# Adding transfers issued by GpSimd make the low halves of plainly split weights, in place of subtractions on VectorE

## The chip, the cores and the metric

The kernel runs on one core of one Trainium2 chip. The metric is device microseconds (us) of one execution. The kernel before took 1804.53, 1805.53 and 1805.5 us in three runs, median 1805.5 us.

## What is computed

Two transformer blocks, one after the other, on 512 positions of width 1024, all in float32 (the reference in JAX, cut):

```python
# first block
u = rms_norm(h, attn_pre_norm[i])
c_q, c_kv, k_rope, m_q, m_k, m_v, m_o, m_i, m_f = split_cols(u @ w_in[i], IN_SIZES)
...
mix = jnp.concatenate([mla_out, mlstm_out], axis=-1) @ w_out[i]
h = h + rms_norm(mix, attn_post_norm[i])
f = rms_norm(h, ffn_pre_norm[i])
f = (jax.nn.silu(f @ w_gate[i]) * (f @ w_up[i])) @ w_down[i]
h = h + rms_norm(f, ffn_post_norm[i])
h = h + jax.nn.sigmoid(h @ w_ple_gate[i]) * (p[i] @ w_ple_proj[i])
# second block, on 16 meta positions and these 512
for i in range(2):
    h = _rmsnorm(hres, norm_g[i, 0])
    m = _diff_attention(...) if i == 0 else _short_conv(...)
    hres = hres + _rmsnorm(m, norm_g[i, 1])
    h = _rmsnorm(hres, norm_g[i, 2])
    a = jax.nn.relu(h @ w_up[i])
    hres = hres + _rmsnorm((a * a) @ w_down[i], norm_g[i, 3])
```

## The kernel before, in words

**Split products.** TensorE multiplies in a reduced format (F32R). So that the product is good to float32, each weight and each activation is kept as two F32R halves, high and low (`x = hi + lo`), and `mm3` (lines 344, 345 and 346) issues three matmuls per tile: weight high by activation high, weight high by activation low, weight low by activation high. Line 346 alone reads a weight's low half.

**The weights.** They lie in HBM as float32, in pieces of [128, 1024] (768 wide for the last down projection of the first block). `loader` brings them in the order of use: each half of a piece, 128x512 or 256 KB, goes by one DMA that SP issues (`dma`, line 325) into one of six `raw` buffers. `converter` follows in the same order: ACT copies `raw` into the weight's high half, in F32R (`copy`, line 289), and a small stream of its own, `convert_lo`, makes the low half as `raw - hi` (`lo`, which calls `tt`, line 303; the planner gives it to VectorE, DVE, or to GpSimd, POOL). Then `convert_lo` gives the `raw` buffer back, and after both halves the weight counts as made. A made weight lies in one of five buffers `whl` or, while their pool is open, one of four buffers `whx`. PE frees it with its last matmul on it (`drop`). Some weights of the three FFNs are not split in this plain way but as "pair" or "part" pieces (`convert_pair`, `part`), which make their low halves in their own code.

**The stages.** `s.phase` is 0 in the first block up to its mixer's output, 1 from `block1_rest` on (output projection, SwiGLU FFN), and 2 from the gate `ple` on (per-layer gate, differential attention, squared-ReLU FFN, short convolution, squared-ReLU FFN).

**The order of the work.** All of it is planned in Python before anything is emitted. Every piece of work is a generator that yields requests for an engine with a cost in us, or for a key or a buffer; `Sched.step` takes the request that can start first (then by priority), and the instruction is emitted there. So each engine has one fixed order, and in it an instruction waits for its semaphores, and what stands behind it on that engine waits too. `s.port` is the planner's lock between POOL and those DVE operations that read two operands from SBUF.

In `ple` (the gate at the end of the first block) ACT computes a sigmoid from each gate projection `t`; DVE multiplies it with the projection `u` and frees `u` for PE. In `converter` the copies stand where the planner put them among the other work of ACT: squares for the norms (`sqt`), activations' high halves (`a`), moves from PSUM (`y`).

```python
    def convert_lo(s, name, lo, raw, hi, left, x):
        yield from s.lo(lo, raw, hi)
        s.put("raw")
        left[0] -= 1
        if not left[0] and ("w", name) not in s.keys:
            s.set(("w", name))
```

Of the kernel before, what the change touches and what calls it, by code (L numbers as in the profile page):

```python
# [10 lines left out]
F32 = mybir.dt.float32  # L11
# [3 lines left out]
ALU = mybir.AluOpType  # L15
# [69 lines left out]
class Sched:  # L85
# [84 lines left out]
    def start(s, st):  # L170
        r = st.req
        if r[0] == "vg":
            d, p = max(st.at("dve"), s.free["dve"]), max(st.at("pool"), s.free["pool"], s.port)
            if r[3]:
                d = max(d, s.port)
            return (p, "pool", r[2]) if p + r[2] <= d + r[1] + 0.2 else (d, "dve", r[1])
        cost = r[1] * (1.07 if r[0] == "pe" else 1.0)
        if r[0] == "act" and len(r) > 2 and r[2] in s.TABLES and r[2] not in s.SERVES[s.table]:
            cost += 1.28
        a = max(st.at(r[0]), s.free[r[0]])  # L180
        if r[0] == "pool" or r[0] == "dve" and r[-1] is True:
            a = max(a, s.port)
        return a, r[0], cost

    def step(s):
        best = None
        for st in s.ready:
            a, eng, cost = s.start(st)
            late = 0.5 if eng == "act" and cost > 1.28 and s.table else 0.0
            k = (a + late, st.prio() if callable(st.prio) else st.prio, st.t, st.seq)  # L190
            if best is None or k < best[0]:
                best = k, st, a, eng, cost
        if best is None:
            return False
        _, st, a, eng, cost = best
        s.ready.remove(st)
        s.now = a
        s.free[eng] = a + cost
        if (eng == "pool" or eng == "dve" and st.req[-1] is True):
            s.port = a + cost  # L200
        st.t = st.end = a + cost + LAT
        st.last = eng
        value = eng
        if eng == "act" and len(st.req) > 2 and st.req[2] in s.TABLES and st.req[2] not in s.SERVES[s.table]:
            s.table = s.TABLES[st.req[2]]
            value = "load"
        s.advance(st, value)
        return True
# [39 lines left out]
class Kern(Sched):  # L248
# [93 lines left out]
    def mm3(s, ps, wh, wl, xh, xl, start, stop, **k):  # L342
        mm = s.nc.tensor.matmul
        mm(ps, wh, xh, start=start, stop=False, **k)  # L344
        mm(ps, wh, xl, start=False, stop=False, **k)  # L345
        mm(ps, wl, xh, start=False, stop=stop, **k)  # L346
# [16 lines left out]
    def mm(s, ps, l, r, start=True, stop=True, passes=1):  # L363
        yield "pe", passes * size(ps) / 2400
        s.nc.tensor.matmul(ps, l, r, start=start, stop=stop)  # L365
# [84 lines left out]
    def converter(s):  # L450
        for i, (name, src, n) in enumerate(s.wq):
            if name[0][0] == "da":
                yield "key", "x_closed"
            if name[0][1:] == ("up", 0, 0) and not name[1]:
                s.reserve()
            more = i + 1 < len(s.wq) and s.wq[i + 1][0][0][1] in ("pair", "part")
            if name[0][1] == "pair":
                if name[1]:
                    yield from s.convert_pair(name[0], more)
                continue  # L460
            if name[0][1] == "part":
                yield "key", ("raw", name, 0)
                yield from s.part(name, s.raw.pop((name, 0)), True, more)
                continue
            yield "key", ("raw", name, 0)
            w, kind = yield from s.w_room()
            s.w[name] = (w, kind)
            s.wn += 1
            left = [len(range(0, n, 512))]
            for x in range(left[0]):  # L470
                m = min(512, n - 512 * x)
                yield "key", ("raw", name, x)
                raw = s.raw.pop((name, x))[:, :m]
                hi, lo = (w[:, j, 512 * x:512 * x + m] for j in range(2))
                yield from s.copy(hi, raw)
                low = s.convert_lo(name, lo, raw, hi, left, x)
                if i:
                    s.spawn(low)
                else:
                    yield from low  # L480
                    s.set(("w+", name) if x else ("w", name))

    def convert_lo(s, name, lo, raw, hi, left, x):
        yield from s.lo(lo, raw, hi)
        s.put("raw")
        left[0] -= 1
        if not left[0] and ("w", name) not in s.keys:
            s.set(("w", name))
# [1891 lines left out]
```

## Time and profile before

| | before |
|---|---|
| median of three runs | 1805.5 us (1804.53 to 1805.53) |
| profiled execution: its own time | 1807.18 us |
| profiled execution: span of the trace | 1805.4 us |
| PE (matmul) busy | 1780.7 us, 99% |
| DVE busy | 1358.4 us, 75% |
| ACT busy | 1008.2 us, 56% |
| POOL busy | 169.8 us, 9% |
| transfers issued by SP | 169.73 MB, 29.4% of the 16 DMA engines' span |

The profile was taken from one execution; all stretches below are of that one. PE is TensorE's matmul pipe, DVE VectorE, ACT ScalarE, POOL GpSimd, SP the engine that issues the DMAs before. A row of the timeline gives the start in us from the start of the span, the length in us, engine, line, operation, the program's names (buffer numbers left out), the shape and how many instructions of a kind in a row; what stands in brackets is the idle time just before and what ended it.

### The profile page before, as it was taken

The numbers are of one execution on the slowest core, as the hardware profiler recorded it, in microseconds if no ns is written. First come the engines' busy times: TensorE is split into PE (matmuls) and PEld (weight loads), VectorE is DVE, ScalarE is ACT, GpSimd is POOL, SyncE is SP. The second block draws the span as 40 slices with busy tenths as digits, with TensorE's granted clock in tenths as the row PEclk, the third lists the DMA queues.
The fourth block names the chain that finished last, engine by engine and source line by source line (L and its number), as shares of the span: only waits on it lengthen the run. The fifth ranks groups of instructions, "written<-read, shape, count | busy, mean of one in ns | idle before, by whom it ended". The sixth has DMA issues, their size and how long they took to land.

```text
span 1805.4 us, 33466 instructions
## 1 busy us (share of the span) xinstructions
PE 1780.7 (99%) x12610; PEld 1658.2 (92%) x12610; DVE 1358.4 (75%) x3066; ACT 1008.2 (56%) x2280; POOL 169.8 (9%) x193
## 2 busy tenths in 40 slices
PE   9999999999999999999999999999999999999997
PEld 7888898999999989999999999999999988889997
DVE  7878579788887858887596777787855378777784
ACT  8767666544445546776675444455522467444452
POOL 2021001000010102111000000001000000111100
PEclk9999999999999999999999999999999999999999
DMA  5324411333325321111222333332422032333331
GB/s 193 96 83 135 148 59 67 116 100 106 106 91 161 106 62 60 60 60 61 68 76 90 98 101 106 99 122 81 146 93 91 23 100 77 101 112 98 105 106 47
DMA packets 96219, 171.87 MB, mean 95 GB/s; under 512 B 12000, under 2 KB 15760, under 8 KB 96056
## 3 DMA queue, kind: packets, MB, share of 16 engines
q1 hardware_dynamic: 96056, 169.73, 29.4%
q8 instruction: 99, 1.62, 0.4%
q14 instruction: 64, 0.52, 0.1%
HBM read 165.92 MB, written 2.13 MB: 93 GB/s over the span
## 4 chain that ended last, share of the span: by engine, by line
PE 92%; DVE 5%; ACT 1%; DMA 1%; issue 1%; SPq 0%; DVEq 0%; ACTq 0%
PE u L344 17%; PE u L345 17%; PE u L346 17%; PE t L345 12%; PE t L346 12%; PE t L344 12%; PE t L2012 1%; DVE whl L303 1%; DVE ssum L303 1%; PE t L765 1%; DVE a L316 1%; DVE y L316 1%; DVE h L303 0%; PE t L365 0%; ACT y L289 0%
## 5 line engine op out<-in xcount | busy, mean ns | idle before, releaser
L344 PE MATMUL u<-a,whl 128*128 128x256 f32 (+3 forms) x1860 | 594.0, 319 | 1.8 <-ACT a L289 0.9
L346 PE MATMUL u<-a,whl 128*128 128x256 f32 (+3 forms) x1860 | 588.0, 316 | 0.0
L345 PE MATMUL u<-a,whl 128*128 128x256 f32 (+3 forms) x1860 | 587.4, 316 | 0.3 <-DVE a L316 0.3
L289 ACT ACTIVATE whl<-raw 128x512 fp32r<-128x512 f32 (+1 forms) x658 | 387.6, 622 | 323.0 <-PE u L346 133.3
L303 DVE TENSOR_TENSOR whl<-raw,whl 128x512 fp32r<-128x512 f32 x625 | 430.1, 708 | 129.6 <-ACT whl L289 127.4
L344 PEld LDWEIGHTS u<-a,whl 128*128 128x128 f32 x1860 | 351.5, 189 | 28.3 <-ACT a L289 1.4
L345 PEld LDWEIGHTS u<-a,whl 128*128 128x128 f32 x1860 | 350.6, 188 | 25.2 <-DVE a L316 1.5
L346 PEld LDWEIGHTS u<-a,whl 128*128 128x128 f32 x1860 | 350.7, 189 | 22.9
L344 PE MATMUL t<-a,whl 128*128 128x256 f32 (+3 forms) x888 | 260.1, 293 | 1.0 <-DVE t L308 0.8
L346 PE MATMUL t<-a,whl 128*128 128x256 f32 (+3 forms) x888 | 259.2, 292 | 0.0
L345 PE MATMUL t<-a,whl 128*128 128x256 f32 (+3 forms) x888 | 258.9, 292 | 0.0
L345 PE MATMUL t<-T,whl 128*128 128x256 f32 (+1 forms) x656 | 185.6, 283 | 0.0
L344 PE MATMUL t<-T,whl 128*128 128x256 f32 (+1 forms) x656 | 184.7, 282 | 0.1
L346 PE MATMUL t<-T,whl 128*128 128x256 f32 (+1 forms) x656 | 184.5, 281 | 0.0
L344 PEld LDWEIGHTS t<-a,whl 128*128 128x128 f32 x888 | 167.4, 188 | 6.3 <-issue 1.2
L345 PEld LDWEIGHTS t<-a,whl 128*128 128x128 f32 x888 | 167.0, 188 | 4.9
L346 PEld LDWEIGHTS t<-a,whl 128*128 128x128 f32 x888 | 167.0, 188 | 3.4
L308 DVE TENSOR_TENSOR y<-y,u 128x258 f32<-128x258 f32 (+2 forms) x192 | 96.7, 506 | 68.6 <-PE u L346 68.4
L344 PEld LDWEIGHTS t<-T,whl 128*128 128x128 f32 x656 | 124.0, 189 | 0.3 <-DVE e L308 0.3
L346 PEld LDWEIGHTS t<-T,whl 128*128 128x128 f32 x656 | 124.0, 189 | 0.0
L345 PEld LDWEIGHTS t<-T,whl 128*128 128x128 f32 x656 | 123.7, 189 | 0.0
L303 DVE TENSOR_TENSOR ssum<-ssum,sqt 128x256 f32<-128x256 f32 (+3 forms) x146 | 66.5, 460 | 57.1 <-ACT sqt L289 54.8
(313 smaller groups left out, 2860.1 us busy)
## 6 DMA issues: line engine op xcount, KB each, us to landing
raw<-in_w_up SPq DMA_DIRECT2D x172, 256.0 KB, 2.9
raw<-in_w_dn SPq DMA_DIRECT2D x168, 256.0 KB, 2.8
raw<-in_w_in SPq DMA_DIRECT2D x128, 256.0 KB, 2.9
raw<-in_w_out SPq DMA_DIRECT2D x48, 256.0 KB, 2.6
raw<-in_w_gate SPq DMA_DIRECT2D x44, 256.0 KB, 2.6
h<-in_xT SPq DMA_DIRECT2D x16, 256.0 KB, 4.3
raw<-in_w_pleg SPq DMA_DIRECT2D x16, 256.0 KB, 3.1
bc<-rows_dram SPq DMA_DIRECT2D x4, 640.0 KB, 3.6
```

Source lines behind the costliest of these rows:

```text
L289: s.nc.scalar.activation(out, in_, f, **k)
L303: (s.nc.gpsimd if e == "pool" else s.nc.vector).tensor_tensor(out, a, b, op)
L308: s.nc.vector.tensor_tensor(out, a, b, op)
L316: s.nc.vector.scalar_tensor_tensor(out, a, c, b, op0, op1)
L344: mm(ps, wh, xh, start=start, stop=False, **k)
L345: mm(ps, wh, xl, start=False, stop=False, **k)
L346: mm(ps, wl, xh, start=False, stop=stop, **k)
L765: s.nc.tensor.transpose(ps[:, (i - j) * P:(i - j + 1) * P], al[i][:, c + j * P:c + (j + 1) * P], s.ident)
L2012: mm(banks[c][-1][0], q[r, e, qs], k[r, f, a:b], start=x == 0, stop=x == 2)
```

## The change

From phase 1 on, `converter` calls `convert_lo_dma` in place of `convert_lo`. It gives the `raw` buffer back at once, lets ACT write minus the high half into the low half, and lets POOL issue a DMA that reads the same piece of the weight from HBM a second time and adds it onto what is there: `-hi + w`. The planner counts 0.9 us of POOL for the issue and 3.5 us until the half is made, and does not take the port lock for it. The "pair" and "part" pieces stay as they were.

```diff
--- before.py
+++ after.py
@@ -178,7 +178,7 @@
         if r[0] == "act" and len(r) > 2 and r[2] in s.TABLES and r[2] not in s.SERVES[s.table]:
             cost += 1.28
         a = max(st.at(r[0]), s.free[r[0]])
-        if r[0] == "pool" or r[0] == "dve" and r[-1] is True:
+        if r[0] == "pool" and r[-1] != "issue" or r[0] == "dve" and r[-1] is True:
             a = max(a, s.port)
         return a, r[0], cost
 
@@ -196,7 +196,7 @@
         s.ready.remove(st)
         s.now = a
         s.free[eng] = a + cost
-        if (eng == "pool" or eng == "dve" and st.req[-1] is True):
+        if (eng == "pool" and st.req[-1] != "issue" or eng == "dve" and st.req[-1] is True):
             s.port = a + cost
         st.t = st.end = a + cost + LAT
         st.last = eng
@@ -473,7 +473,10 @@
                 raw = s.raw.pop((name, x))[:, :m]
                 hi, lo = (w[:, j, 512 * x:512 * x + m] for j in range(2))
                 yield from s.copy(hi, raw)
-                low = s.convert_lo(name, lo, raw, hi, left, x)
+                if s.phase:
+                    low = s.convert_lo_dma(name, lo, raw, hi, src[:, 512 * x:512 * x + m], left, x)
+                else:
+                    low = s.convert_lo(name, lo, raw, hi, left, x)
                 if i:
                     s.spawn(low)
                 else:
@@ -483,6 +486,18 @@
     def convert_lo(s, name, lo, raw, hi, left, x):
         yield from s.lo(lo, raw, hi)
         s.put("raw")
+        left[0] -= 1
+        if not left[0] and ("w", name) not in s.keys:
+            s.set(("w", name))
+
+    def convert_lo_dma(s, name, lo, raw, hi, src, left, x):
+
+        s.put("raw")
+        yield from s.copy(lo, hi.bitcast(F32), scale=-1.0)
+        yield "pool", 0.9, "issue"
+        s.nc.gpsimd.dma_start(lo, src, accum_op=ALU.add)
+        s.cur.t += 3.5
+        yield "wait", 0.0
         left[0] -= 1
         if not left[0] and ("w", name) not in s.keys:
             s.set(("w", name))
```

By the instruction lists, DVE has 3066 rows before and 2828 now, POOL 193 and 431, ACT gains 256 copies, SP's and PE's instructions stay the same in number. 256 adding DMAs are issued, 248 of 128x512 (256 KB) and 8 of 128x256 (128 KB). They concern 128 pieces: 4 of the 8 of the first block's output projection; 10 gate and up pieces and the 8 last down pieces of its FFN; 10 of the gate `ple`; 24 and 24 of the projections into differential attention and short convolution; 8 and 8 of their output projections; 8 and 8 first up pieces and 8 and 8 last down pieces of the two squared-ReLU FFNs.

**At the gate `ple`, ACT.** `whl<-raw` is a copy to a high half, `whl<-whl` the new write of minus the high half, `t<-t` the sigmoid. Before:

```order
L289 ACTIVATE whx_6932<-raw_7007 128x512
L289 ACTIVATE whl_7106<-raw_7022 128x512
L289 ACTIVATE whl_7106<-raw_7030 128x512
L289 ACTIVATE whl_7118<-raw_7039 128x512
L289 ACTIVATE whl_7118<-raw_7048 128x512
L289 ACTIVATE whl_7134<-raw_7054 128x512
L289 ACTIVATE whl_7134<-raw_7063 128x512
L289 ACT_TABLE_LOAD
L289 ACTIVATE t_7114<-t_6817 128x512
L289 ACTIVATE t_7128<-t_6818 128x512
L289 ACTIVATE t_7147<-t_6819 128x512
```

Now (the last 12 rows of this run of conversions; six more copies of the same kind stand ahead):

```order
L289 ACTIVATE whl_7182<-whl_7182 128x512
L289 ACTIVATE whl_7208<-raw_6955 128x512
L289 ACTIVATE whl_7182<-whl_7182 128x512
L289 ACTIVATE whl_7208<-raw_6989 128x512
L289 ACTIVATE whl_7208<-whl_7208 128x512
L289 ACTIVATE whl_7219<-raw_7179 128x512
L289 ACTIVATE whl_7208<-whl_7208 128x512
L289 ACTIVATE whl_7219<-raw_7181 128x512
L289 ACTIVATE whl_7219<-whl_7219 128x512 x2
L289 ACT_TABLE_LOAD
L289 ACTIVATE t_7176<-t_6883 128x512
L289 ACTIVATE t_7191<-t_6884 128x512
```

Before the table load stand 6 copies to `whl` in a row; now it stands behind 16 copies, for four weights in place of three.

**At the output projection of differential attention, its sixth piece, PE with the semaphores that each row waits for.** Before:

```order
L344 MATMUL u_10902<-a_8009,whx_10871 128x258 [waits DMAHW2_49,DMAHW1_49,DMAHW3_49,Activation_49,Pool_49]
L345 MATMUL u_10902<-a_8009,whx_10871 128x258
L346 MATMUL u_10902<-a_8009,whx_10871 128x258 [waits DVE_49]
L344 MATMUL u_10902<-a_8352,whx_10871 128x258
L345 MATMUL u_10902<-a_8352,whx_10871 128x258
```

Now:

```order
L344 MATMUL u_11047<-a_8288,whx_10993 128x258 [waits DMAHW3_49,DMAHW2_49,DMAHW4_49,Activation_49,Pool_49]
L345 MATMUL u_11047<-a_8288,whx_10993 128x258
L346 MATMUL u_11047<-a_8288,whx_10993 128x258 [waits DMASW2_49]
L344 MATMUL u_11047<-a_8489,whx_10993 128x258
L345 MATMUL u_11047<-a_8489,whx_10993 128x258
```

The first matmul that reads the low half, line 346, waited for DVE; now it waits for a DMA issued by POOL (DMASW). On ACT the conversions at this place stood like this before:

```order
L289 ACTIVATE a_10818<-y_10808 128x256
L289 ACTIVATE whx_10871<-raw_10351 128x512
L289 ACTIVATE whx_10871<-raw_10359 128x512
L289 ACTIVATE y_10876<-u_10610 128x258
L289 ACTIVATE whx_10882<-raw_10467 128x512
L289 ACTIVATE y_10880<-u_10624 128x258
L289 ACTIVATE whx_10882<-raw_10492 128x512
```

and now:

```order
L289 ACTIVATE a_10940<-y_10930 128x256
L289 ACTIVATE whx_10993<-raw_10452 128x512
L289 ACTIVATE whx_10993<-raw_10460 128x512
L289 ACTIVATE whx_10993<-whx_10993 128x512
L289 ACTIVATE whx_11006<-raw_10575 128x512
L289 ACTIVATE whx_10993<-whx_10993 128x512
L289 ACTIVATE whx_11006<-raw_10597 128x512
L289 ACTIVATE whx_11006<-whx_11006 128x512
L289 ACTIVATE whx_11029<-raw_10758 128x512
L289 ACTIVATE whx_11006<-whx_11006 128x512
```

The first low half was DVE's work behind the first copy; now it is ACT's third copy here, and the second low half its fifth.

**At the start of the second squared-ReLU FFN, ACT.** The fourth of the four pieces with which that FFN begins is `whl_17959` before and `whl_18229` now. Before:

```order
L289 ACTIVATE y_17765<-u_17908 128x256
L289 ACTIVATE a_17955<-h_2194,V 128x256
L289 ACTIVATE a_17969<-h_2195,V 128x256
L289 ACTIVATE a_17978<-h_2196,V 128x256
L289 ACTIVATE whl_17959<-raw_17555 128x512
L289 ACTIVATE whl_17959<-raw_17566 128x512
L289 ACTIVATE y_17795<-u_17953 128x256
L289 ACTIVATE a_18002<-h_2197,V 128x256
```

Now:

```order
L289 ACTIVATE whl_18131<-raw_17741 128x512
L289 ACTIVATE whl_18131<-whl_18131 128x512
L289 ACTIVATE y_18010<-u_18177 128x256
L289 ACTIVATE whl_18229<-raw_18057 128x512
L289 ACTIVATE sqt_18237<-y_17980 128x256
L289 ACTIVATE whl_18131<-whl_18131 128x512
L289 ACTIVATE sqt_18242<-y_18010 128x256
L289 ACTIVATE whl_18229<-raw_18075 128x512
L289 ACTIVATE whl_18229<-whl_18229 128x512
L289 ACTIVATE whl_18253<-raw_18107 128x512
L289 ACTIVATE whl_18229<-whl_18229 128x512
```

Its low half needs ACT's row `whl_18229<-whl_18229`, and the low halves of the three pieces ahead of it stand on ACT as well.

## Rows read from the trace of the kernel before

**Rows 1.** Page: engines' busy time over the span; shares of the chain that ended last.

```profile
PE 1780.7 (99%) x12610; PEld 1658.2 (92%) x12610; DVE 1358.4 (75%) x3066; ACT 1008.2 (56%) x2280; POOL 169.8 (9%) x193
...
PE 92%; DVE 5%; ACT 1%; DMA 1%; issue 1%; SPq 0%; DVEq 0%; ACTq 0%
```

**Rows 2.** Windows: stretch, length, busy PE PEld DVE ACT POOL, clock, DMA share, GB/s.

```profile
200.00:1805.40 1605.40, 1585.35 (x11684) 1496.88 (x11683) 1199.97 (x2730) 859.41 (x1993) 130.70 (x131) 1.00 0.29 91
...
1260.00:1400.00 140.00, 138.98 (x1001) 130.98 (x1000) 93.96 (x173) 50.71 (x94) 1.30 (x1) 1.00 0.33 110
```

**Rows 3.** Waits of PE: what for, us in total, times, longest.

```profile
PE m L365 <- DVE ssum L303: 5.4, 3, 3.0
```

**Rows 4.** Groups by form: busy us, mean ns of one, then idle time before.

```profile
L289 ACT ACTIVATE whl<-raw 128x512 fp32r<-128x512 f32 x654 | 386.1, 623 | 323.0 <-PE u L346 133.3 <-DVE raw L303 87.1 <-PE t L346 39.9
...
L303 DVE TENSOR_TENSOR whl<-raw,whl 128x512 fp32r<-128x512 f32 x623 | 429.3, 709 | 129.6 <-ACT whl L289 127.4
...
L303 POOL TENSOR_TENSOR whl<-raw,whl 128x512 fp32r<-128x512 f32 x31 | 45.2, 1464 | 429.6 <-ACT whl L289 292.2 <-DVE t L303 130.9 <-issue 6.6
...
L1134 POOL MEMSET y<- 128x3 f32 x4 | 0.4, 103 | 0.0
```

**Rows 5.** DMA: the SP queue's packets, MB, share; issues, KB, median us to landing.

```profile
q1 hardware_dynamic: 96056, 169.73, 29.4%
...
raw<-in_w_in SPq DMA_DIRECT2D x128, 256.0 KB, 2.9
raw<-in_w_out SPq DMA_DIRECT2D x48, 256.0 KB, 2.6
...
raw<-in_w_ukv SPq DMA_DIRECT2D x2, 256.0 KB, 4.8
```

**Rows 6.** Timeline at the gate `ple`, 613 to 620 us.

```profile
613.79 3.24 ACT L289 ACTIVATE whl<-raw 128x512 fp32r<-128x512 f32 x6 [4.17 <-PE t L346]
...
615.17 3.34 SPq L325 DMA_DIRECT2D raw<-in_w_in  x6
...
617.04 1.28 ACT L289 ACT_TABLE_LOAD   x1
618.34 1.58 ACT L289 ACTIVATE t<-t 128x512 f32<-128x512 f32 x3
...
618.97 1.28 DVE L308 TENSOR_TENSOR t<-t,u 128x512 f32<-128x512 f32 x2 [0.81 <-ACT t L289]
...
619.71 0.50 PE L344 MATMUL u<-a,whl 128*128 128x512 f32 x1 [0.76 <-DVE t L308]
```

**Rows 7.** Timeline at the sixth piece of the attention's output projection.

```profile
874.33 1.14 ACT L289 ACTIVATE whx<-raw 128x512 fp32r<-128x512 f32 x2
...
874.97 4.20 DVE L303 TENSOR_TENSOR whx<-raw,whx 128x512 fp32r<-128x512 f32 x6
...
876.65 0.28 PE L346 MATMUL u<-a,whx 128*128 128x258 f32 x1
```

**Rows 8.** Window and timeline at the start of the second squared-ReLU FFN.

```profile
1436.00:1451.00 15.00, 12.00 (x100) 11.74 (x99) 14.90 (x38) 13.00 (x32) 0.00 (x0) 1.00 0.18 56
...
1444.54 1.14 ACT L289 ACTIVATE whl<-raw 128x512 fp32r<-128x512 f32 x2
...
1447.80 0.68 DVE L303 TENSOR_TENSOR whl<-raw,whl 128x512 fp32r<-128x512 f32 x1
...
1448.87 0.70 PE L365 MATMUL m<-ssum,ones 128*128 128x256 f32 x2 [3.00 <-DVE ssum L303]
...
1450.70 0.28 PE L346 MATMUL t<-a,whl 128*128 128x256 f32 x1
```

**Rows 9.** Timeline: first squared-ReLU FFN, first last-down pieces, low half and its readers.

```profile
1206.04 0.89 DVE L303 TENSOR_TENSOR whl<-raw,whl 128x512 fp32r<-128x512 f32 x1
...
1215.19 0.28 PE L346 MATMUL u<-a,whl 128*128 128x258 f32 x1
...
1217.72 0.29 PE L346 MATMUL u<-a,whl 128*128 128x258 f32 x1
```

## The prediction, made before the changed kernel was run

> **What bounds the kernel now.** I first read the page's list of engines and its chain of work: PE is busy for 1780.7 of 1805.4 us, and 92% of the chain that ended last is PE's own work [rows 1]. The windows say where the rest is: from 200 us to the end, which holds all that the change touches, PE lacks 1605.4 - 1585.4 = 20.0 us in all [rows 2]. So nothing that is taken from another engine can give back more than these 20 us, while everything that makes PE wait is paid in full. The table of waits then shows what PE waits for: the largest entry is the sum for a norm on DVE, 5.4 us in three waits [rows 3]. Weights are no entry of size: the low halves come in time, made by DVE in 709 ns each [rows 4], and it is the spare time of each weight, from the end of its low half to PE's first matmul on line 346, that decides what the change costs. I looked that up in the timelines of the places where a stage begins or ends.
>
> **The change, part by part.** It takes 244 subtractions of at most 0.71 us from DVE and 12 of at most 1.46 us from POOL [rows 4]. DVE is busy 75% of the time [rows 1] and mostly beside PE, so most of these 170 us are worth nothing. It adds 256 copies to ACT, 256 DMA issues to POOL, and some 66 MB of reads. ACT has 1008 us of work [rows 1], and at about 0.52 us each (the second of two copies ends 1.14 - 0.62 us behind the first [rows 4, 7]) gains 133 us: no bound on the average. POOL has 170 us; also none.
>
> The path of one low half becomes longer. Before: copy, then 0.7 us on DVE. Now: copy, a second copy on ACT, an issue on POOL, a landing. Nothing in the trace shows an issue by POOL. Its nearest rows are a tiny POOL memset of 0.10 us and a 128x512 operation of 1.46 us [rows 4]; I take 1.0, since SP's six issues in a row took 3.34 us, 0.56 each [rows 6], and POOL's own small work stands between the two ends. Nothing shows an adding transfer either. A plain 256 KB load lands in 2.6 to 2.9 us, the slowest group in 4.8 [rows 5]. All of SP's transfers, 169.73 MB, took 29.4% of 1805.4 us of the 16 engines [rows 5], so 256 KB take 0.82 us of them. An adding one must also read what lies in SBUF. I take 2.9 + 0.82 = 3.7 us, with bounds of 2.6 (as a plain one) and 5.8 (two plain ones, one behind the other). Issue and landing together: 4.7 us, between 2.7 and 7.3.
>
> The Trainium skill ("DMA: Bandwidth & Descriptors", section "Anatomy of one DMA — SWDGE (gpsimd) path") puts a transfer issued by GpSimd at 2.0 us plus its bytes over 436 GB/s, an estimate of 2.6 us for 256 KB; it says nothing there of an addition, and no run here shows it yet. With 2.6 in place of 3.7 the sum below would be 2.2 us less, 1822.
>
> In the long projections, weights are converted far ahead and 4 us more are hidden. The places that are not covered:
>
> *Gate `ple`.* ACT does six copies from 613.79 in 3.24 us, then a table load, then the sigmoids at 618.34; DVE follows at 618.97, and PE, out of work, restarts at 619.71 behind DVE after 0.76 us without work [rows 6]. There is no spare time in this chain. Now 16 copies stand ahead of the table load, 10 more at 0.52: **+5.2 us**, whatever the transfers do. The first of them still waits for PE to free a buffer, as the 4.17 us of idle time before the six show [rows 6].
>
> *Sixth output piece of the attention.* Its copies begin at 874.33, DVE's subtractions at 874.97, and PE reads the first low half at 876.65 [rows 7], about 1.0 us after it was made. Now the low half is ACT's third copy: 874.33 + 3 x 0.52 + 0.1 = 876.0; plus 4.7 gives 880.7, **+4.0** late (bounds 2.05 with 2.7, 6.6 with 7.3). The second low half, ACT's fifth copy, is covered by that wait.
>
> *Start of the second squared-ReLU FFN.* The fourth piece's first copy ended at 1444.54 + 0.62 = 1445.16, PE reads the low half at 1450.70, and ACT was busy 13.0 of the 15 us to 1451 [rows 8]. Before, that copy was the fifth of these pieces in this stretch (the first piece had been made earlier); now its low half needs the fifteenth. Ten more copies are 5.2 us, less 2.0 us of idle time if all of that can be used: 1448.4 to 1450.4, I take 1449.4. Plus 4.7: 1454.1, **+3.4** (bounds 0.4 and 7).
>
> *The last eight down pieces of each FFN.* They come in a burst. The first low half was made at 1206.93 and read at 1215.19, and the next piece is read 2.53 us later [rows 9]: for 16 low halves there are 8.26 + 7 x 2.53 = 26 us. If an adding transfer holds the engines as long as a plain one, 16 x (0.82 + 0.82) = 26.2 us just go in: 0. If it holds them twice as long, 16 x (0.82 + 1.64) = 39.4 us, +13. The second such FFN is the same, and the SwiGLU FFN's eight narrower pieces I price alike: 0 to +40 in all. I take **+7**, near the plain transfer, which is the only one that rows show.
>
> The Trainium skill ("Collectives: The Full Stack", section "The bandwidth ceiling: the fold count and why AG ≠ RS ≠ AR") explains a reduction by DMA as two source reads with two descriptors per chunk, twice the read traffic of a copy; it is told there of rings between cores, and no row here shows it. By that rule the bursts would cost the +40, and the time would be 1857.
>
> *Gain.* Where a norm's sum stands on DVE behind subtractions, it comes earlier: one of 0.68 us at 1447.80 stands just ahead of the sums for which PE waits 3.00 us until 1448.87 [rows 8]. Two or three such places: **-1.5** (bounds 0 and -4, most of the 5.4 us [rows 3]).
>
> Sum: 5.2 + 4.0 + 3.4 + 7 - 1.5 = +18.1 us. Durations are of the profiled execution, whose own time was 1807.18 us, 1.7 above the median; against the median of 1805.5 the forecast is 1823.6, **1824 us**. With all terms at their low ends +3.7 (1809), at their high ends +59 (1864).
>
> **The rivals.** *Throughput of the adding transfers decides.* For: they come in bursts, share 16 engines with the loads, and must read and write the same bytes. Against: the average load is low, 29.4% and at most twice 256 x 0.82 us more. It decides from 26 / 16 = 1.6 us per transfer on. At 1.64 us of engine time the bursts give +40, so 1857; if each goes only behind the landing of the one before, at 2.9, each burst is 46 - 26 = 20 late, 60 in all, and with the other places 1877. At 3.7 even the 24 pieces of the short convolution, 48 halves in these 140 us [rows 2], would be late by 38, and the time over 1930. Chance 0.20, a third of it above 1872.
>
> *Faster: DVE's relief outweighs the path.* At the gate, the 4.17 us of ACT's idle time [rows 6] would take eight of the added copies if buffers came free earlier, since `raw` is given back sooner: 1.0 left of 5.2. Issue and landing are 2.7: +2.05 and +0.4, bursts 0. With half of the 20 us that PE lacks [rows 2] gained through earlier norms and moves on DVE, the sum is 3.5 - 10 = -6.5: 1799. It decides once the gain exceeds those 3.5 us by 3.6. Against: the copies waited for PE, not for `raw`, and only 5.4 us of PE's waits are DVE's sums. Chance 0.07.
>
> *Absorbed.* The same low prices with a gain of 4: -0.5, so 1805. Chance 0.06. That the change does not do what it says I leave out: the instruction lists show every subtraction gone and every DMA in place.
>
> **How the numbers follow.** The forecast's chance is 0.67, its own range 1809 to 1857. A difference of 0.2%, 3.6 us, is about what a measurement of this kernel tells from none. Faster 0.07, within 0.06, slower 0.67 + 0.20 = 0.87. The range 1809 to 1872 leaves out the two cases below it, 0.13, and the top of the throughput rival, 0.07.
>
> **What would show it.** At the gate: 16 copies in some 8.4 us ahead of the table load, and PE's wait for DVE grown from 0.76 to about 6 us. At the sixth output piece and at the start of the second squared-ReLU FFN: waits on line 346 for the adding DMA, 3 to 4 us each. In the bursts: waits on line 346 at several pieces in turn, small ones by the forecast, each of 1 us or more by the rival. In the list of DMA issues: landings of the adding ones near 3.7 us, and a new queue's share of the engines of 256 x 0.82 / 1805 = 12%, or double that. The forecast is wrong if PE's new idle time lies in the long projections, or if the landing is above 6 us or below 2.6.

## The result, and the profile after

The changed kernel takes 1866.65 us (median of three runs, 1861.78 to 1869.25) against 1805.5: the ratio is 1.0332, 95% interval 1.0317 to 1.0347. It is slower by 61 us, over three times the 18 us of the forecast, and inside the range given. The profiled execution has a span of 1864.9 us.

The page's engines and the chain that ended last, of the changed kernel (to be held against [rows 1]):

```profile
PE 1799.4 (96%) x12610; PEld 1669.9 (90%) x12610; DVE 1220.9 (65%) x2828; ACT 1127.5 (60%) x2536; POOL 365.7 (20%) x431
...
PE 78%; issue 7%; ACT 5%; DVE 4%; DMA 4%; POOL 1%; SPq 0%; POOLq 0%; DVEq 0%; ACTq 0%
```

DVE has lost 137 us of work, where the forecast had some 170, and ACT gained 119, where it had 133. PE's idle time has grown from 24.7 to 65.5 us, by 40.8. The other 18.7 us of the longer span are the same 12610 matmuls taking longer: a matmul that follows a wait is drawn longer (0.55 us at 910.65 below, 0.28 in [rows 7]), and some run at a lower clock (last section).

The queues' shares and some rows of the list of DMA issues, of the changed kernel (compare [rows 5]; q0 is GpSimd's, q1 SP's):

```profile
q1 hardware_dynamic: 96056, 169.73, 27.8%
q0 software_dynamic: 36864, 66.08, 21.4%
...
raw<-in_w_in SPq DMA_DIRECT2D x128, 256.0 KB, 4.1
whl<-in_w_in POOLq DMA_DIRECT2D x78, 256.0 KB, 4.9
...
whl<-in_w_dn POOLq DMA_DIRECT2D x20, 256.0 KB, 6.6
```

SP's 256 KB take 27.8% x 1864.9 / 169.73 x 0.262 = 0.80 us of the 16 engines. An adding 256 KB take 21.4% x 1864.9 / 66.08 x 0.262 = **1.58 us**, double. Landings are 4.7 to 6.6 us by group (medians), where I took 3.7. Away from the bursts it is no less: in e11_mid below, which adds in the long projections alone, GpSimd's queue took 8.2% of 1807.9 us for 23.60 MB, 1.65 us per 256 KB.

PE's waits of the changed kernel, the largest (what for, us in total, times, longest; compare [rows 3]):

```profile
PE u L346 <- DMA whl<-in_w_dn: 9.1, 14, 1.0
PE u L344 <- DVE t L308: 6.0, 1, 6.0
PE t L346 <- DMA whl<-in_w_up: 5.9, 2, 3.3
PE m L642 <- ACT sqt L289: 4.9, 1, 4.9
PE m L365 <- DVE ssum L303: 4.7, 3, 2.9
PE u L344 <- issue: 4.6, 1, 4.6
PE u L346 <- DMA whx<-in_w_dn: 3.2, 6, 1.1
```

From top to bottom: the bursts of last down pieces; the gate; the start of the second squared-ReLU FFN; a norm just ahead of the gate, which I had not foreseen; the old wait for a norm's sum, unchanged; the sixth output piece; the bursts again. Line 642 is line 627 of the kernel before.

### The profile page after: what moved, and what is told of

The parts are those of the page before. It is cut to its first block, busy times and chain, and to the rows that moved or that the text cites. A ratio compares the mean times of both kernels' runs of the same rounds, so it can differ in the third digit from the quotient of the medians.

```text
span 1864.9 us, 33901 instructions
## 1 busy us (share of the span) xinstructions
PE 1799.4 (96%) x12610; PEld 1669.9 (90%) x12610; DVE 1220.9 (65%) x2828; ACT 1127.5 (60%) x2536; POOL 365.7 (20%) x431
## 3 DMA queue, kind: packets, MB, share of 16 engines
q1 hardware_dynamic: 96056, 169.73, 27.8%
q0 software_dynamic: 36864, 66.08, 21.4%
## 4 chain that ended last, share of the span: by engine, by line
PE 78%; issue 7%; ACT 5%; DVE 4%; DMA 4%; POOL 1%; SPq 0%; POOLq 0%; DVEq 0%; ACTq 0%
PE u L346 14%; PE u L344 14%; PE u L345 14%; PE t L345 11%; PE t L346 11%; PE t L344 11%; ACT whl L289 2%; ACT whx L289 1%; DMA whx<-in_w_dn 1%; POOL whl L498 1%; DVE p L754 1%; DMA whl<-in_w_up 1%; PE t L780 1%; DMA whx<-in_w_out 1%; DVE y L316 1%
## 5 line engine op out<-in xcount | busy, mean ns | idle before, releaser
L344 PE MATMUL u<-a,whl 128*128 128x256 f32 (+3 forms) x1828 | 583.1, 319 | 8.1 <-DVE t L308 6.0
L346 PE MATMUL u<-a,whl 128*128 128x256 f32 (+3 forms) x1828 | 579.0, 317 | 10.8 <-DMA whl<-in_w_dn 9.1
L345 PE MATMUL u<-a,whl 128*128 128x256 f32 (+3 forms) x1828 | 576.1, 315 | 0.3 <-DVE a L316 0.3
L303 DVE TENSOR_TENSOR whl<-raw,whl 128x512 fp32r<-128x512 f32 x443 | 312.0, 722 | 101.6 <-ACT whl L289 100.3
L346 PEld LDWEIGHTS u<-a,whl 128*128 128x128 f32 x1828 | 345.6, 189 | 36.7 <-DMA whl<-in_w_dn 11.9
L344 PEld LDWEIGHTS u<-a,whl 128*128 128x128 f32 x1828 | 346.1, 189 | 33.7 <-DVE t L308 6.4
L345 PEld LDWEIGHTS u<-a,whl 128*128 128x128 f32 x1828 | 345.6, 189 | 23.1 <-issue 1.0
L346 PE MATMUL t<-a,whl 128*128 128x256 f32 (+2 forms) x928 | 273.8, 295 | 8.2 <-DMA whl<-in_w_up 5.9
L344 PE MATMUL t<-a,whl 128*128 128x256 f32 (+2 forms) x928 | 274.9, 296 | 3.0 <-DVE t L308 3.0
L345 PE MATMUL t<-a,whl 128*128 128x256 f32 (+2 forms) x928 | 273.4, 295 | 0.0
L346 PEld LDWEIGHTS t<-a,whl 128*128 128x128 f32 x928 | 177.3, 191 | 12.5 <-DMA whl<-in_w_up 6.5
L344 PEld LDWEIGHTS t<-a,whl 128*128 128x128 f32 x928 | 177.9, 192 | 8.6 <-issue 3.3
L344 PE MATMUL t<-T,whl 128*128 128x256 f32 (+1 forms) x656 | 184.7, 282 | 0.3 <-DVE e L308 0.3
L345 PEld LDWEIGHTS t<-a,whl 128*128 128x128 f32 x928 | 177.4, 191 | 5.4
L308 DVE TENSOR_TENSOR y<-y,u 128x258 f32<-128x258 f32 (+2 forms) x192 | 96.8, 507 | 107.9 <-PE u L346 107.8
L344 PEld LDWEIGHTS t<-T,whl 128*128 128x128 f32 x656 | 124.0, 189 | 0.6 <-DVE e L308 0.6
```

The source lines that it names most:

```text
L303: (s.nc.gpsimd if e == "pool" else s.nc.vector).tensor_tensor(out, a, b, op)
L308: s.nc.vector.tensor_tensor(out, a, b, op)
```

## The experiments

All are made from the changed kernel. The kernel before ran beside each group at medians of 1806.9 to 1807.4 us; ratios are to that.

**Plain loads in place of additions (e1_plain).**

```diff
-        s.nc.gpsimd.dma_start(lo, src, accum_op=ALU.add)
+        s.nc.gpsimd.dma_start(lo, src.bitcast(F32R))
```

> The changed kernel with the addition taken out of the 256 DMAs: GpSimd issues the same transfers as plain loads (the low halves then hold the whole weight), and every instruction of every engine keeps its place. Theory A (load: an adding transfer holds the 16 engines twice as long as a plain one, 1.58 us against 0.80 per 256 KB by the two queues' shares in the profile after, and in the bursts transfers queue for the engines): the share of the GpSimd queue falls from 21.4% to about 11%, landings from 5 to 6 us to about 3, the waits of line 346 in the bursts (some 16 us) and at the gate's start (7.5 us) nearly vanish, and the time is 1820 to 1838 us. Theory B (path: the copy on ACT, the issue of 0.9 us and the fixed part of a landing make the low halves late, whatever the transfer does with the data): 1852 to 1867 us.

1828.72 us, ratio 1.0119 (1.0104 to 1.0134): 21.6 above the kernel before. So about 39 of the 61 us go with the addition. Not all of that is waiting: of the 41.3 us between the two profiled spans (1864.9 and 1823.6), 15.4 are PE's busy time (1799.4 and 1784.0). GpSimd's queue falls to 13.0% of the engines, 0.94 us per 256 KB; the landings, still 3.4 to 6.6 us, fall less than I expected. The window over the first burst (stretch, length, busy PE, PEld, DVE, ACT, POOL, clock, DMA share, GB/s), first of the changed kernel:

```profile
555.00:585.00 30.00, 25.44 (x204) 24.20 (x203) 11.41 (x27) 23.72 (x56) 13.83 (x16) 1.00 1.00 242
```

and with plain loads:

```profile
555.00:585.00 30.00, 29.13 (x239) 28.45 (x239) 12.99 (x31) 25.08 (x57) 10.03 (x19) 1.00 1.05 320
```

In both the 16 engines are full (a share a little over 1 comes from packets that overlap), but with additions they bring 242 GB/s instead of 320, and PE loses 4.6 of 30 us instead of 0.9. The gate's wait stays at 6.0 us and the sixth output piece's at 4.6: these two are not the addition's. At the start of the second squared-ReLU FFN 4.3 of the 5.9 us stay.

**Which stages pay (e2_long, e3_down, e4_edge).** The condition for the adding transfer is narrowed to one group of weights each:

```diff
-                if s.phase:
+                if s.phase and name[0][0] in ("da", "sc"):                                # e2_long
+                if s.phase and name[0][1] == "down":                                      # e3_down
+                if s.phase and name[0][0] not in ("da", "sc") and name[0][1] != "down":   # e4_edge
```

> Adding transfers only for the 48 pieces of the two long projections (into differential attention and short convolution); all other low halves by subtraction as before. Both theories: these pieces are converted 20 us and more ahead, so the time is that of the kernel before within 4 us, 1802 to 1809 us. If the long stages themselves cost something (Theory C: contention with all other work, spread over the stages), 1815 us or more.

> Adding transfers only for the 24 last down pieces of the three FFNs, 48 halves in three bursts; all other low halves by subtraction. Theory A (load): 16 halves of 0.80 + 1.58 us each need 38 us of the engines where PE gives 26, so waits of line 346 stay in the bursts: +12 to +20, 1817 to 1826 us. Theory B (path): some 8 us of spare time cover the 5 to 6 us of the longer path: 1804 to 1811 us.

> Adding transfers for all pieces but those of the long projections and the last down pieces: the output projections, the plain up pieces at the start of each FFN, the gate ple, 112 halves. Both theories put the late weights at the gate (5 us and its start), the sixth output piece (4 to 6) and the start of the second squared-ReLU FFN (6 to 7) here, with the clock's loss after them. Theory A: the gate's start and the first FFN's start are relieved since the burst of down pieces no longer fills the engines just before: +20 to +35, 1826 to 1841 us. Theory B: all of the loss is here, +45 to +61, 1850 to 1867 us.

e2_long 1814.72 us (1.0046, 1.003 to 1.0062), e3_down 1829.98 (1.0127, 1.0112 to 1.0142), e4_edge 1835.2 (1.0158, 1.0141 to 1.0175): +7.6, +22.8 and +28.1 us over the kernel before beside them, 58.5 in all, nearly the 61. The 48 halves of the bursts cost nearly as much as the 112 of e4_edge; the 96 of the long projections, a third as much as either or less. e3_down cost more than the 12 to 20 us that I expected, and e2_long missed my expectation. The reason stands in its timeline: PE's wait at the gate was 4.9 us, since three of the four pieces converted there are the first head's projections, which this kernel makes by addition.

**The long projections without those three pieces (e11_mid).**

```diff
-                if s.phase:
+                if s.phase and (name[0][0] == "sc" or name[0][0] == "da" and name[0][1] > 0):
```

> Adding transfers only for the long projections without the three pieces that are converted at the gate (the first head's), 45 pieces; the rest by subtraction. The run with all 48 was 7.6 us above the kernel before, with PE's wait at the gate at 4.9 us where it was 0.8. Theory D (ACT's copies ahead of the table load): 1805 to 1811 us, the gate's wait at about 1 us. If the long stages cost the 7.6 us themselves: 1812 to 1817 us. A gain by DVE's relief would show as less than 1803 us.

1809.35 us, ratio 1.0008 (0.9999 to 1.0017): no loss that can be told from none, and no gain. 90 subtractions off DVE bought nothing that shows, and 90 additions far ahead of their use cost none, though they landed after 5.1 to 6.5 us. The gate's wait was 0.8 us.

**ACT's copies without transfers (e5_copy).**

```diff
-        s.put("raw")
         yield from s.copy(lo, hi.bitcast(F32), scale=-1.0)
-        yield "pool", 0.9, "issue"
-        s.nc.gpsimd.dma_start(lo, src, accum_op=ALU.add)
-        s.cur.t += 3.5
-        yield "wait", 0.0
+        yield from s.tt(lo, lo.bitcast(F32), raw, ALU.add)
+        s.put("raw")
```

> No adding transfers at all: ACT still writes minus the high half into the low half, and DVE (or GpSimd) then adds the raw half onto it from SBUF; raw is given back after that. So this holds the 256 copies on ACT and the order that they give it, without the transfers. Theory D (order on ACT: the added copies stand ahead of the table load at the gate and, at the sixth output piece, ahead of the moves out of the PSUM tiles u that PE waits for): PE's wait on line 344 of 5 to 6 us at the gate and 4 to 5 us at the sixth output piece are there as in the changed kernel, +10 to +16, 1817 to 1823 us. If those two waits are the adding transfers' (landing), they are gone here: 1805 to 1811 us.

1830.94 us, ratio 1.0134 (1.0119 to 1.0149), +24: more than expected, and without a single adding transfer. Its two waits, word for word:

```profile
PE u L344 <- DVE t L308: 6.0, 1, 6.0
PE u L344 <- issue: 4.2, 1, 4.2
```

They are the gate's and the sixth output piece's. So both belong to the order on ACT. They are 9.4 of the 24 us beyond what was there before; PE's busy time is another 7.8 (1788.5 against 1780.7), and the rest is small waits, on DVE above all. At the gate the wait follows the number of conversion copies ahead of the table load, over five kernels: 6 copies 0.8 us (before), 10 copies 2.8 (e4_edge), 12 copies 3.9 (e10_rawlate, below), 14 copies 4.9 (e2_long), 16 copies 6.0 (the change), 0.52 us each. At the sixth output piece the timeline of the changed kernel shows what PE waited for:

```profile
908.54 0.61 ACT L289 ACTIVATE whx<-raw 128x512 fp32r<-128x512 f32 x1
909.07 1.13 ACT L289 ACTIVATE whx<-whx 128x512 fp32r<-128x512 f32 x2
910.10 0.18 ACT L289 ACTIVATE dummy<-eps 128x1 f32<-128x1 f32 x1
910.20 0.90 ACT L289 ACTIVATE y<-u 128x258 f32<-128x258 f32 x3
...
910.65 0.55 PE L344 MATMUL u<-a,whx 128*128 128x258 f32 x1 [4.55 <-issue]
...
912.16 0.58 PE L346 MATMUL u<-a,whx 128*128 128x258 f32 x1 [0.73 <-DMA whx<-in_w_out]
```

PE begins its next output in a tile `u` as soon as ACT has moved the first old one out (`y<-u`). These moves stood between the conversions before; now they stand behind all twelve of them. The adding transfer itself makes PE wait only 0.73 us more.

**Minus the high half by DVE (e9_neg_dve).**

```diff
-        yield from s.copy(lo, hi.bitcast(F32), scale=-1.0)
+        yield "dve", 0.07 + size(lo) / 960
+        s.nc.vector.tensor_scalar(lo, hi.bitcast(F32), -1.0, 0.0, ALU.mult, ALU.add)
```

> The changed kernel with minus the high half written by DVE in place of ACT; the adding transfers stay, 256 of them. Theory D (order on ACT): the waits at the gate (6 us) and at the sixth output piece (4.7 us on line 344) shrink to about 1 and 0 to 4 us, while the waits of the bursts stay: 10 to 16 less than the changed kernel, 1851 to 1857 us. If ACT's copies cost nothing and all is the transfers: 1863 to 1869 us.

1876.85 us, ratio 1.0379 (1.0355 to 1.0404): slower than the change, against my expectation. The gate's wait did shrink, to 2.6 us, and line 344 no longer waits at the sixth output piece. But two others grew:

```profile
PE m L365 <- DVE ssum L303: 14.9, 6, 4.1
PE u L346 <- DMA whx<-in_w_out: 9.7, 4, 6.9
```

The sums of the norms are later; some stand on DVE among 256 writes more, some on GpSimd among its issues (15 of them there, 3 in the change), and which of the two made them late I did not separate. And the sixth piece, no longer held up by ACT, waits for its adding transfer instead, 6.9 us. Two waits had lain one over the other there; taking one away showed the other.

**The second read alone (e12_load).** Plain loads as in e1_plain, and no copy on ACT to the low half:

```diff
-        yield from s.copy(lo, hi.bitcast(F32), scale=-1.0)
...
-        s.nc.gpsimd.dma_start(lo, src, accum_op=ALU.add)
+        s.nc.gpsimd.dma_start(lo, src.bitcast(F32R))
```

> Plain loads by GpSimd (no addition) and no copies on ACT to the low half: the second read of each weight alone, planned anew without the copies (the low halves hold the whole weight). If the 61 us are the addition's load on the engines (some 39 us, by the run with plain loads) plus the order that ACT's copies bring (some 20 us), with both taken out nothing of size is left: 1805 to 1813 us, the gate's wait back at about 1 us and no wait of 4 us on line 344 at the sixth output piece. If the longer path of GpSimd's issue and landing costs much by itself: 1820 us or more.

1816.38 us, ratio 1.0049 (1.0035 to 1.0063), +9.0: slightly above my expectation, and far below the 61. The gate's wait did not go back to 1 us; only eight copies stand ahead of the table load, but the last two waited for loads from HBM (2.70 and 0.73 us):

```profile
624.79 0.63 ACT L289 ACTIVATE whl<-raw 128x512 fp32r<-128x512 f32 x1 [2.70 <-DMA raw<-in_w_in]
626.15 0.63 ACT L289 ACTIVATE whl<-raw 128x512 fp32r<-128x512 f32 x1 [0.73 <-DMA raw<-in_w_in]
```

**GpSimd's queue (e6_nopool).** From phase 1 on, the planner gives no addition or subtraction to GpSimd:

```diff
-            return (p, "pool", r[2]) if p + r[2] <= d + r[1] + 0.2 else (d, "dve", r[1])
+            return (p, "pool", r[2]) if not s.phase and p + r[2] <= d + r[1] + 0.2 else (d, "dve", r[1])
```

> The changed kernel with all additions and subtractions from phase 1 on kept off GpSimd, so that no sum of a norm stands behind a waiting issue on GpSimd's queue. Theory E (queue: ACT's 8.9 us of idle time until 611.35 us and PE's 4.9 us wait for the norm's square come from an addition to h that stands behind issues on GpSimd): that wait goes, 5 to 9 us less than the changed kernel, 1858 to 1862 us. If the norm there is late for another reason: 1864 to 1870 us.

1855.73 us, ratio 1.0274 (1.0253 to 1.0295), some 11 us less than the change, more than expected. PE's wait of 4.9 us at line 642 is gone, and so is one of 3.0 us in the first block's FFN (`PE t L344 <- DVE t L308`); PE's busy time is 3.9 us less. This is what had happened in the changed kernel (timeline of GpSimd and ACT just ahead of the gate):

```profile
604.72 0.89 POOL L498 DMA_DIRECT2D whl<-in_w_plep  x1 [0.86 <-issue]
607.06 0.88 POOL L498 DMA_DIRECT2D whl<-in_w_plep  x1 [1.45 <-issue]
609.70 0.86 POOL L498 DMA_DIRECT2D whx<-in_w_pleg  x1 [1.76 <-issue]
610.26 1.05 POOL L303 TENSOR_TENSOR h<-h,y 128x256 f32<-128x256 f32 x1
...
611.35 0.72 ACT L289 ACTIVATE a<-h 128x256 fp32r<-128x256 f32 x2 [8.86 <-POOL h L303]
```

The engines are full here (a share of 1.11 from 604 to 610 us), and issues leave GpSimd only every 2.3 to 2.6 us. An addition to `h` stood behind three of them, ACT waited 8.86 us for it, and PE waited for the norm's square that ACT makes from it.

**The planner told the truth (e7_late).**

```diff
-        s.cur.t += 3.5
+        s.cur.t += 6.0
```

> The changed kernel, planned with 6.0 us in place of 3.5 us from an adding transfer's issue to its end, near the measured 5 to 6.6 us. Theory F (wrong figure in the plan): with the true figure the planner puts other work of PE into the waits, 1835 to 1852 us. Theory A (the 16 engines are full in the bursts) and D (copies on ACT): no figure helps, since the order of the weights is fixed; within 7 us of the changed kernel, 1860 to 1873 us.

1869.88 us, ratio 1.0343 (1.0324 to 1.0361): no better. So the wrong landing in the plan is not what costs the time.

**`raw` given back late (e10_rawlate).**

```diff
-        s.put("raw")
         yield from s.copy(lo, hi.bitcast(F32), scale=-1.0)
...
         yield "wait", 0.0
+        s.put("raw")
```

> The changed kernel with one part undone: a raw buffer is given back only when its adding transfer is planned to have ended, as the subtraction did, in place of at once. Theory G (loads of the next pieces, started at once, crowd the adding transfers): fewer loads beside the additions in the bursts, waits of line 346 smaller, 1848 to 1862 us. Theory A (the sum of what a burst must move decides, not who goes first): 1860 to 1876 us, the same or a little more, since loads start later.

1859.5 us, ratio 1.0282 (1.0266 to 1.0298): in the range of Theory G and just below that of Theory A. But the sign that Theory G named did not come. Of the some 8 us, 2.1 are at the gate (12 copies for 16); the waits of line 346 in the bursts are no smaller, 14.2 us where the change has 12.3. So the crowding by early loads is not borne out there; what gave the rest I leave open.

**Load or path (e14_half_down, e15_down_plain).** The bursts alone, as e3_down, with half of the additions, and with none:

```diff
-                if s.phase and name[0][1] == "down":
+                if s.phase and name[0][1] == "down" and not x:      # e14_half_down
```
```diff
-        s.nc.gpsimd.dma_start(lo, src, accum_op=ALU.add)
+        s.nc.gpsimd.dma_start(lo, src.bitcast(F32R))                # e15_down_plain
```

> As the run with adding transfers for the 24 last down pieces alone (22.8 us above the kernel before), but only the first half of each piece is made so; the second half by subtraction. Theory A (what a burst must move decides): 16 loads of 0.80 and 8 additions of 1.58 us are 25.4 us where there are 26, so the waits of line 346 for the adding transfers nearly go, 1806 to 1814 us. Theory B (path: a piece is late when its low half takes copy, issue and landing, however few there are): the first halves, read first, are as late as before, 1822 to 1832 us.

> As the run with adding transfers for the 24 last down pieces alone, with the addition taken out: the same instructions in the same places, plain loads by GpSimd (those low halves hold the whole weight). Theory A: 16 x (0.80 + 0.94) = 28 us per burst, little more than the 26 there are: 1807 to 1815 us. Theory B (path): the issue, the copy on ACT and most of the landing stay, 1822 to 1832 us.

e14_half_down 1809.84 us (1.0018, 1.0009 to 1.0028), e15_down_plain 1810.92 (1.0021, 1.0012 to 1.003), where e3_down had +22.8. The burst of the first squared-ReLU FFN in the windows, the 26 us from about its first down piece on: with all additions (e3_down)

```profile
1215.00:1241.00 26.00, 22.00 (x165) 20.11 (x164) 8.13 (x19) 18.67 (x41) 9.67 (x12) 1.00 1.08 271
```

with half of them (e14_half_down)

```profile
1211.00:1237.00 26.00, 26.00 (x217) 25.93 (x216) 12.85 (x29) 13.80 (x32) 4.85 (x6) 1.00 0.78 210
```

and with plain loads (e15_down_plain):

```profile
1211.00:1237.00 26.00, 25.78 (x212) 25.35 (x211) 9.95 (x23) 17.98 (x40) 6.94 (x14) 1.00 0.94 298
```

The choice of the 26 us does not make the difference: from 1205 to 1250 us PE worked 40.2, 45.0 and 44.8 of 45 us. The landings are not shorter on the whole than in e3_down, 6.7 (`whl`) and 5.3 us (`whx`) in the median there: the halved additions land after 6.2 and 7.1, the plain loads after 4.9 and 6.8. Yet all but 2.5 and 3.6 us of the 22.8 go once there is less to move. In the bursts it is load, not path. One thing goes with the addition besides the engine time, an issue that keeps GpSimd 0.34 us longer; GpSimd was busy 9.67 of the 26 us in e3_down, and this was not tried by itself.

## Why the prediction was wrong, point by point

**What bounds the kernel, and where it would show.** Right: PE was the bound, PE's new waits of size lie where a stage begins or ends, and the long projections hide theirs (e11_mid). Wrong: "everything that makes PE wait is paid in full" was too little. PE's waits grew by 40.8 us, and 18.7 us more came as the same matmuls taking longer, which no term of the sum held. Of the 40.8 us the terms of the sum cover some 28: 12.3 in the bursts, 5.2 at the gate, 5.3 at the sixth piece, 5.9 at the start of the second squared-ReLU FFN, less 0.7 of gain. The rest stood in no term: 4.2 at line 642, 2.2 for the gate's own weights (`whl<-in_w_pleg`), 2.2 in the first block's FFN, and smaller ones. DVE's relief was worth next to nothing: the old wait for norm sums went from 5.4 to 4.7 us, where I had -1.5.

**Gate, +5.2.** Right in mechanism and size: 0.76 to 5.95 us.

```profile
643.88 1.28 ACT L289 ACT_TABLE_LOAD   x1
645.17 1.57 ACT L289 ACTIVATE t<-t 128x512 f32<-128x512 f32 x3
...
646.55 0.79 PE L344 MATMUL u<-a,whl 128*128 128x512 f32 x1 [5.95 <-DVE t L308]
```

**Sixth output piece, +4.0.** The size was near (4.55 + 0.73), the mechanism wrong: it is the moves out of PSUM behind the copies on ACT, shown by e5_copy. The order rows ahead of the prediction had them: `y<-u` between the conversions before, none of them between the conversions now. I followed the weight and not what else stands on ACT's queue.

**Start of the second squared-ReLU FFN, +3.4.** Mechanism right, size off: two waits of line 346, 2.68 and 3.27 us [compare rows 8]:

```profile
1493.73 1.22 PE L365 MATMUL m<-ssum,ones 128*128 128x256 f32 x2 [2.87 <-DVE ssum L303]
...
1499.34 0.39 PE L346 MATMUL t<-a,whl 128*128 128x256 f32 x1 [2.68 <-DMA whl<-in_w_up]
...
1503.23 0.58 PE L346 MATMUL t<-a,whl 128*128 128x256 f32 x1 [3.27 <-DMA whl<-in_w_up]
```

The median landing of `whl<-in_w_up` was 5.7 us, not 3.7, and the pieces were late one after the other. With plain loads 4.3 of the 5.9 us stay (e1_plain), and in e5_copy, without transfers, none: so most of this term is the path by GpSimd's queue, as the forecast had it, and not the addition.

**Bursts, +7: the step that failed.** I put an adding transfer's time on the engines near a plain one's 0.82 us, "the only one that rows show", and so expected the 26 us of a burst to hold its 26.2 us of transfers. Measured, it is 1.58 us, and the burst needs 16 x (0.80 + 1.58) = 38 us. The term, priced at 0 to 40, was +22.8 us by itself (e3_down), and 19 of these go with the addition (e15_down_plain). The engine time shows the cause and not the size: 38 - 26 is 12 us for each burst, but PE waited on line 346 for 14.0 us in all three together (e3_down); the sixteen issues of the second burst there were spread over 34 us (1210.96 to 1244.78), not 26. It did not stay in the bursts either: GpSimd's issues were held back, an addition for a norm stood behind them, and PE waited 4.9 us, which no term of the sum held; keeping all such work off GpSimd gave some 11 us (e6_nopool). In all, the addition accounts for about 39 of the 61 us (e1_plain). For the 19 in the bursts it is shown that this is load on the engines; for the other 20 only that they go with the addition. Of the 22 that stay, the gate's 5.2 and the sixth piece's 4.6 are ACT's order.

The Trainium skill ("Collectives: The Full Stack", section "The bandwidth ceiling: the fold count and why AG ≠ RS ≠ AR") explains a reduction by DMA between cores by two source reads per chunk. The trace agrees nearly in engine time: 1.58 us against 0.94 for the same DMAs without the addition, and against SP's 0.80; the second read itself is in no row. By that rule the prediction had 1857, 10 us below what came. That it came so near is in part luck: it had 40 us in the bursts, which cost 22.8 by themselves, and nothing for the longer matmuls and the waits that stood in no term.

**The rivals.** "Throughput of the adding transfers decides", held at 0.20, is what happened in the bursts. Its point of decision, 26 / 16 = 1.6 us per transfer, was worked out wrongly: it leaves out the 16 plain loads that share the engines, and beside them 0.8 us is left for an addition, as the forecast's own sum of 26.2 us says. The measured 1.58 is just under the one and double the other. I named the right rule and the right test, and then weighed them by which rows there were, not by what an addition must do.

**The tests named.** Sixteen copies ahead of the table load: yes. Waits on line 346 in the bursts, small ones or of 1 us and more: 20 waits of 0.6 us on average, 1.1 the longest, which fits neither well. A queue's share of 12% or double that: 21.4%, near the double. Landings near 3.7 us: no, 4.7 to 6.6; five groups are above the 6 us that the prediction had named as a sign that it is wrong. An issue by GpSimd, taken at 1.0 us, was 0.87 to 0.97.

## What to carry to other kernels

A DMA that adds held the engines here twice as long as SP's plain load and 1.7 times as long as the same DMA without the addition, so count a burst in engine time: what it must move, against the time that the reader gives it. Far ahead of its use it cost nothing that shows (e11_mid); near it, at the begin of a stage, it did, outside the bursts too (e4_edge, +28.1 us with its copies on ACT). Taking work off an engine that is not the bound bought nothing here. TensorE's waits cost more here than their own length: the span grew by 59.5 us with 40.8 of new idle time, and the rest is the same matmuls taking longer. When work is added to an in-order engine, look at what is pushed behind it, a table load or the freeing of a PSUM tile, before following the data that it makes; and keep short work that others wait for off a queue that issues DMAs which can be held back.

## What the runs showed of the hardware

An adding 256 KB from HBM held the 16 engines for 1.58 us (1.65 in e11_mid), the same transfer without the addition 0.94, SP's plain load 0.80. Its issue kept GpSimd for 0.87 us, the plain one for 0.53 (e15_down_plain). With the engines full, issues by GpSimd came 2.3 to 2.6 us apart just ahead of the gate; what holds them back there was not tried by itself.

TensorE's granted clock fell behind PE's new idle stretches. Two windows of the changed kernel, just behind such stretches, stand near the lower of the clock's two levels, 1.2 of 2.4 GHz:

```profile
615.00:620.00 5.00, 4.79 (x23) 4.61 (x23) 4.32 (x14) 5.00 (x13) 1.82 (x3) 0.53 0.98 209
1500.00:1505.00 5.00, 1.77 (x8) 1.77 (x9) 5.00 (x15) 2.22 (x6) 2.21 (x3) 0.54 1.06 226
```

PE's timeline at the first of them:

```profile
614.60 0.58 PE L642 MATMUL m<-sqt,ones_r 128*128 128x256 f32 x1 [4.94 <-ACT sqt L289]
615.39 0.58 PE L643 MATMUL m<-sqt,ones_r 128*128 128x256 f32 x1 [0.21 <-DVE sqt L303]
615.77 0.41 PE L344 MATMUL t<-a,whl 128*128 128x256 f32 x1
615.99 0.41 PE L345 MATMUL t<-a,whl 128*128 128x256 f32 x1
```

Behind the wait of 4.94 us matmuls of 256 columns start 0.22 us apart. In the kernel before, a wait of 3.00 us had left the clock at 1.00 [rows 8], and behind it they start 0.12 us apart:

```profile
1449.53 0.28 PE L345 MATMUL t<-a,whl 128*128 128x256 f32 x1
1449.65 0.28 PE L346 MATMUL t<-a,whl 128*128 128x256 f32 x1
```

In the changed kernel the same wait, 2.87 us there (1493.73 above), was followed by the slow pace all the same:

```profile
1495.18 0.41 PE L346 MATMUL t<-a,whl 128*128 128x256 f32 x1
1495.39 0.41 PE L344 MATMUL t<-a,whl 128*128 128x256 f32 x1
```

So some waits are paid twice, as idle time and in slower matmuls behind them, and the length of one wait alone does not tell which. How much of the 18.7 us by which PE's busy time grew is this, I did not separate. The mean granted clock, 0.996 before and 0.986 in the change, gives an estimate of the most that it can be: 1864.9 x 0.014 - 1805.4 x 0.004 = 19 us, less what of the slow stretches PE spent idle.
